# Scores of paged keys run on into the paged-value stage of a hybrid decoder step, with four changes of order

## The chip, the cores and the metric

The kernel runs on one core of one Trainium2 chip. The metric is the device time of one launch in microseconds (us), median of several runs, lower is better. TensorE (PE in the profile) multiplies, VectorE (DVE) and ScalarE (ACT) work element by element, GpSimd (POOL) builds masks, and SyncE (SP) issues nearly all the DMA loads and stores. Each engine works through its own instructions in a fixed order and waits for others by semaphores.

## The reference

One step of one layer. Keys and values of 64 past pages are looked up through a page table; the rest is dense.

```python
def branch_inputs(h, w_in, w_alpha, b_alpha):
    u = h @ w_in                      # 2048 -> q, k, v, gate of 8 heads; q, k, v, gate of 4 GLA heads; rank-16 decay
    log_f = log_sigmoid(ga @ w_alpha + b_alpha) / GLA_TAU

def stick_break_weights(z, mask):
    sp = where(mask, softplus(z), 0.0)
    later = cumsum(sp, reverse=True) - sp
    return where(mask, exp(log_sigmoid(z) - later), 0.0)

def sb_sample(q, k_new, v_new, k_past, v_past, bias):      # 8 requests, 4 new tokens, 1024 past tokens each
    z = concatenate([sb_logits(q, k_past, bias), sb_logits(q, k_new, bias)])
    a = stick_break_weights(z, mask)
    return a[..., :P] @ v_past + a[..., P:] @ v_new

def gla_chunk(S, q, k, v, g):
    ...
def branch_output(o_sb, sg, o_gla, gg, gla_norm_g, w_out):
    mixed = concatenate([o_sb * silu(sg), rms_norm(o_gla) * silu(gg)])
    return mixed @ w_out

# x + rms_norm(branch_output(...)) for 1024 prompt tokens (with 16 learned ones ahead) and for 8 x 4 sample tokens;
# k_past = cache_k[page_table], v_past = cache_v[page_table]: 8 pages of 128 tokens per request, 8 heads of 128
```

## The kernel before, in words

All products are made of three matmuls on values split into a high and a low part. The normalised input, transposed, stays on the chip for the whole run. A projection of 128 output columns (`inproj`) takes eight weight pairs of k-tiles (kk = 0 to 7) by three chunks of tokens. One unit is one chunk of one pair: six matmuls. So a projection has 24 units. Each weight pair is loaded (`wr`), cast to its high part by ScalarE (`wh`) and split into its low part by VectorE (`wl`), each with three buffers: the load of pair i waits for VectorE's split of pair i−3, which waits for TensorE's last matmul of pair i−6.

The stages in order of time: the prologue (to 85 us) loads and transposes the input; eight stick-breaking heads, each with the projections v, k and q and its attention; a low-rank product for the decay; gates 0 to 2; the GLA stage with four heads of k, q and two v projections, then gates 3 and 4 (to some 1503 us); the paged stage, gates 5 to 13 with the products of past values (to some 1750 us); gates 14 and 15; and from some 1800 us the output product, whose 104 weight pieces go through a ring of buffers.

Everything beside a projection is woven between its units by `Weaver` (`W`). A piece of work is a generator; `yield n` puts it aside for n units, `spawn` adds one with a delay. `flush` runs units until no piece is left but those marked lasting, `drain` until none is left at all. The instructions so laid down are then ordered by a scheduler at build time, by priority (weights and evacuations are urgent) and by its own times; what it puts out is the fixed order of each engine. `W.mark` is the last matmul of the latest unit, and a dependency without a semaphore on it (`spread`) keeps an instruction from being ordered ahead of that unit.

`z_feed` makes the scores of the past keys. There are 512 steps, one per head, request and page: a load of 64 KB (`kp`, 128 keys of one head) and four VectorE instructions (`jk`, one for each new token) that multiply with a broadcast query (`qb`) and sum. The number of the page is read from the table on SyncE with a register load ahead of the DMA (`page_dma`). A request's row of eight pages goes out to DRAM (`zd`). In the kernel before one page is taken every 2 units from the heads on, three loads ahead in three buffers, and all are done before the paged stage.

In the paged stage, `chain(b)` reads request b's scores back (`dz`) and makes its stick-breaking weights `dA`; `paged_values` loads its eight pages of values, 512 KB each (`vr`, six buffers, issued four pages ahead), and multiplies them (`dO`). `new_keys` adds the new tokens' own part (`Cs`, `Cn`). A request's products can't start before its scores of all heads are there.

In a head, q is taken out of PSUM by ScalarE (`q`, high part, L620) and, straight from PSUM too, by VectorE (low part, L621); the next projection's first matmuls (`acc_v`, or `acc_ga` after the last head) need the PSUM buffer. In the GLA stage a key tile is transposed by token (`by_token`, tile `tr_k`) and a packed copy of 32 of its columns is transposed too (`packed`, tile `trp_k`, copied out as `pk`), both through one PSUM buffer.

Of the kernel before, what the change touches and what calls it, by code (L numbers as in the profile page):

```python
# [10 lines left out]
F32 = mybir.dt.float32  # L11
F32R = mybir.dt.float32r
# [8 lines left out]
P = 128  # L21
# [29 lines left out]
class Weaver:  # L51
# [3 lines left out]
    def __init__(self):  # L55
        self.now, self.n, self.live, self.heap, self.mark = 0, 0, 0, [], None
# [20 lines left out]
    def drain(self):  # L77
        while self.heap:
            self.beat()
# [3 lines left out]
def hybrid_step(ctx: ExitStack, tc: tile.TileContext, x_prompt, x_sample, cache_k, cache_v, state_gla,  # L83
# [195 lines left out]
    def inproj(c0, evac, lo0, nm, chunks=CHUNKS):  # L279

        acc = [accp.tile([P, 512], F32, tag="acc", name=f"acc_{nm}_{c}") for c in range(3)]
        for kk in range(NK // 2):
            wh, wl = weight_chunk(w_in[0], kk, c0, f"{nm}_{kk}")
            for c, (lo, hi) in enumerate(chunks):
                lo = max(lo, lo0)
                n = hi - lo
                for k2 in range(2):
# [3 lines left out]
                    W.mark = mm(acc[c][:, :n], wl[:, k2, :], hh[k][:, lo:hi], start=False, stop=(k == NK - 1)).ins  # L291
                if kk == NK // 2 - 1:
                    with urgent():
                        evac(c, acc[c][:, :n], lo, hi)
# [32 lines left out]

    dk_cm = tc.tile_pool(name="dk", bufs=2, side="right")
# [17 lines left out]
    heads_ready = []  # L346
    z_done = set()

    def z_feed(rate):
# [8 lines left out]
        def fetch(h, b, i):  # L358
            if i == 0:
                qbs[h, b] = dk.tile([P, NT, P], F32, tag="qb", bufs=2, name=f"qb{b}_{h}")  # L360
                nc.sync.dma_start(qbs[h, b][:], qsd[b * NT:(b + 1) * NT, h * P:(h + 1) * P].partition_broadcast(P))
            kps[h, b, i] = dk.tile([P, P], F32, tag="kp", bufs=3, name=f"kp{b}_{h}_{i}")
# [5 lines left out]
        for n, (h, b, i) in enumerate(pages()):  # L368
            while h not in heads_ready:
                yield 4  # L370
            while fetched < n + 3:
# [7 lines left out]
            if i == 0:  # L379
                zt = dk.tile([P, NT, NPG], F32, tag="zt", name=f"zt{b}_{h}")  # L380
            kp = kps.pop((h, b, i))
            for t in range(NT):
                jk = dk.tile([P, P], F32, tag="jk", bufs=1, name=f"jk{b}_{h}_{i}_{t}")
# [10 lines left out]
    def spread(ins):  # L394

        if W.mark is not None:
            tc.add_manual_dep(ins.ins, W.mark.name, NOSYNC, reason="spread")
# [46 lines left out]
    with tc.tile_pool(name="sp", bufs=1) as sp, tc.tile_pool(name="sps", bufs=1, space=PSUM) as sps:  # L444
# [134 lines left out]
        def head(h):  # L579
# [37 lines left out]
            def ev_q(c, ps, lo, hi):  # L617
                e = min(hi, REAL)
                a, b_, n = lo - META, e - META, e - lo
                act.activation(qt[0][:, a:b_], ps[:, :n], AF.Copy, scale=QSCALE)  # L620
                vec.scalar_tensor_tensor(qt[1][:, a:b_], ps[:, :n], QSCALE, qt[0][:, a:b_].bitcast(F32), ALU.mult, ALU.subtract)  # L621
                if hi > REAL:
                    act.activation(qsm[:], ps[:, n:], AF.Copy, scale=QSCALE)
                    W.spawn(sample_q(h, qsm, ks), 5)
# [4 lines left out]
        W.spawn(z_feed(lambda n: 2), lasting=True)  # L629
# [7 lines left out]
        for g in range(3):  # L637
            gate_group(g)
# [3 lines left out]
    with tc.tile_pool(name="gp", bufs=1) as gp, tc.tile_pool(name="gps", bufs=1, space=PSUM) as gps:  # L642
# [51 lines left out]
        def level_masks():  # L694

            yield 12
            for m in (64, 32, 16, 8, 4, 2, 1):
                nb = P // (2 * m)
                a = stage(f"lv{m}")[:, :P]
# [16 lines left out]
        def decay(g, cb):  # L716

            raw = stage(f"walr{g}")[:96, :P]
            for i in range(6):
# [823 lines left out]
```

## Time and profile before

| | us |
|---|---|
| median of 3 runs | 2154.19 (2152.64 to 2156.18) |
| profiled execution | 2153.79 |
| its span | 2152.1 |
| TensorE busy | 2078.1 (97%) |
| VectorE busy | 1572.5 (73%) |
| ScalarE busy | 993.1 (46%) |
| the 2048 `jk` instructions | 590.5 and 166.1 for reading their sums |
| VectorE busy from 840 to 1500 | 557.25 of 660 |
| VectorE busy from 1540 to 1750 | 86.08 of 210 |

The share of busy time says which engine sets the pace of a stage, and the list of TensorE's waits says what it stood for. The granted clock is given for each stretch of time; at 0.50 TensorE runs at half its speed. A busy row in parentheses has the number of instructions.

### The profile page before, as it was taken

How to read it: one execution, taken by the hardware profiler on the slowest of the kernel's cores; microseconds unless marked ns; L12 is line 12 of the kernel's file. 1: busy time of each engine (PE TensorE's matmuls, PEld its weight loads, DVE VectorE, ACT ScalarE, POOL GpSimd, SP SyncE). 2: the span in 40 equal slices, each digit the busy share in tenths (PEclk: the TensorE clock that was granted, in tenths of full speed). 3: DMA queues.
4: the chain of work that ended last, by engine and by line, in shares of the span. 5: the costliest groups of instructions: out<-in, count | busy, mean ns of one | idle time of the engine just before them, and what ended most of it. 6: DMA issues, size and time to landing. Idle time of an engine off the chain costs nothing.

```text
span 2152.1 us, 43331 instructions
## 1 busy us (share of the span) xinstructions
PE 2078.1 (97%) x12546; PEld 1872.8 (87%) x12546; DVE 1572.5 (73%) x6592; ACT 993.1 (46%) x2536; POOL 83.2 (4%) x298
## 2 busy tenths in 40 slices
PE   5999999999999999999999999999999999999997
PEld 5999999998999979998899898998788887777765
DVE  6368889888898879788788887977544347453575
ACT  7345556564655546432534435343443336332342
POOL 0000010000000010020000000000000000000000
PEclk9999999999999999999999999999999999999999
DMA  6125554554555453442343434335776766452485
GB/s 196 52 70 137 139 158 134 161 146 140 149 152 157 135 142 113 124 100 75 107 106 84 117 80 112 97 83 138 221 228 221 222 200 210 130 158 76 128 277 178
DMA packets 380802, 304.02 MB, mean 141 GB/s; under 512 B 50770, under 2 KB 321042, under 8 KB 380562
## 3 DMA queue, kind: packets, MB, share of 16 engines
q1 hardware_dynamic: 378370, 300.97, 48.0%
q8 instruction: 99, 1.62, 0.3%
q14 instruction: 141, 1.16, 0.2%
q10 hardware_dynamic: 2192, 0.27, 0.1%
HBM read 243.39 MB, written 57.72 MB: 140 GB/s over the span
## 4 chain that ended last, share of the span: by engine, by line
PE 71%; DVE 12%; DMA 10%; ACT 3%; issue 3%; SPq 1%; POOL 0%; DVEq 0%; ACTq 0%; POOLq 0%
DVE jk L384 5%; PE acc_g L289 4%; PE acc_g L291 4%; PE acc_g L290 4%; PE b L1452 4%; PE b L1453 4%; PE b L1454 4%; DMA kp<-in_cache_k_dram 3%; PE acc_k L289 3%; PE acc_k L290 3%; PE acc_k L291 3%; PE acc_gv L289 2%; PE acc_gv L291 2%; PE acc_gv L290 2%; PE acc_q L289 2%
## 5 line engine op out<-in xcount | busy, mean ns | idle before, releaser
L384 DVE SCALAR_TENSOR_TENSOR jk<-kp,qb 128x128 f32<-128x128 f32 x2048 | 590.5, 288 | 90.2 <-DMA kp<-in_cache_k_dram 51.8
L289 PE MATMUL acc_g<-hT,wh_g 128*128 128x304 f32 (+2 forms) x768 | 253.8, 330 | 5.1 <-ACT gx L438 4.7
L291 PE MATMUL acc_g<-hT,wl_g 128*128 128x368 f32 (+2 forms) x768 | 248.0, 323 | 0.0
L290 PE MATMUL acc_g<-hT,wh_g 128*128 128x304 f32 (+2 forms) x768 | 247.9, 323 | 0.0
L289 PEld LDWEIGHTS acc_g<-hT,wh_g 128*128 128x128 f32 x768 | 144.9, 189 | 31.9 <-ACT wh_g L184 12.1
L1452 PE MATMUL b<-ring,f 128*128 128x512 f32 x416 | 165.8, 400 | 3.4 <-ACT b L1351 1.6
L1316 DVE TENSOR_TENSOR ring<-wr,ring 128x512 fp32r<-128x512 f32 x104 | 70.6, 689 | 133.0 <-ACT ring L1315 132.5
L384 DVE DVE_READ_ACCUMULATOR jk<-kp,qb 128x1 f32 x2048 | 166.1, 81 | 0.1
L1453 PE MATMUL b<-ring,f 128*128 128x512 f32 x416 | 162.5, 391 | 0.7 <-DVE ring L1316 0.7
L1454 PE MATMUL b<-ring,f 128*128 128x512 f32 x416 | 162.2, 390 | 0.0
L291 PEld LDWEIGHTS acc_g<-hT,wl_g 128*128 128x128 f32 x768 | 145.0, 189 | 1.6 <-issue 1.6
L290 PEld LDWEIGHTS acc_g<-hT,wh_g 128*128 128x128 f32 x768 | 145.1, 189 | 0.7
L1315 ACT CAST ring<-wr 128x512 fp32r<-128x512 f32 x104 | 64.0, 621 | 162.9 <-DMA wr<-in_w_out_dram 80.9
L512 ACT ACTIVATE X<-X 127x512 f32<-127x512 f32 (+4 forms) x112 | 54.9, 491 | 165.2 <-DVE X L511 165.1
L289 PE MATMUL acc_gv<-hT,wh_gv 128*128 128x384 f32 (+1 forms) x384 | 130.1, 339 | 0.0
L289 PE MATMUL acc_k<-hT,wh_k 128*128 128x378 f32 (+1 forms) x384 | 127.6, 332 | 0.0
L291 PE MATMUL acc_gv<-hT,wl_gv 128*128 128x384 f32 (+1 forms) x384 | 126.0, 328 | 0.0
L289 PE MATMUL acc_q<-hT,wh_q 128*128 128x368 f32 (+2 forms) x384 | 125.4, 326 | 0.0
L290 PE MATMUL acc_k<-hT,wh_k 128*128 128x378 f32 (+1 forms) x384 | 125.4, 326 | 0.0
L291 PE MATMUL acc_k<-hT,wl_k 128*128 128x378 f32 (+1 forms) x384 | 125.2, 326 | 0.0
L290 PE MATMUL acc_gv<-hT,wh_gv 128*128 128x384 f32 (+1 forms) x384 | 125.2, 326 | 0.0
L290 PE MATMUL acc_q<-hT,wh_q 128*128 128x368 f32 (+2 forms) x384 | 123.6, 322 | 0.0
(427 smaller groups left out, 5483.4 us busy)
## 6 DMA issues: line engine op xcount, KB each, us to landing
kp<-in_cache_k_dram SPq DMA_DIRECT2D x512, 64.0 KB
vr<-in_cache_v_dram SPq DMA_DIRECT2D x64, 512.0 KB
qb<-qsd SPq DMA_DIRECT2D x64, 256.0 KB
tf<-in_w_out_dram SPq DMA_DIRECT2D x64, 256.0 KB
td<-tf SPq DMA_DIRECT2D x64, 256.0 KB
wr_g<-in_w_in_dram SPq DMA_DIRECT2D x128, 128.0 KB
wr<-td SPq DMA_DIRECT2D x64, 256.0 KB
wr<-in_w_out_dram SPq DMA_DIRECT2D x48, 256.0 KB
```

Source lines behind the costliest of these rows:

```text
L289: mm(acc[c][:, :n], wh[:, k2, :], hh[k][:, lo:hi], start=(k == 0), stop=False)
L290: mm(acc[c][:, :n], wh[:, k2, :], hl[k][:, lo:hi], start=False, stop=False)
L291: W.mark = mm(acc[c][:, :n], wl[:, k2, :], hh[k][:, lo:hi], start=False, stop=(k == NK - 1)).ins
L384: ins = vec.scalar_tensor_tensor(jk[:], kp[:], 1.0, qbs[h, b][:, t, :], ALU.mult, ALU.mult, accum_out=zt[:, t, NPG - 1 - i:NPG - i])
L512: act.activation(X, X, AF.Exp)
L1315: act.copy(wh, r)
L1316: vec.tensor_tensor(wl, r, wh.bitcast(F32), ALU.subtract)
L1452: mm(bk[:], ah, wh, start=first and k == 0, stop=False, skip_group_check=True)
L1453: mm(bk[:], ah, wl, start=False, stop=False, skip_group_check=True)
L1454: mm(bk[:], al, wh, start=False, stop=last and k == 7, skip_group_check=True)
```

## The change

It has five parts.

1. `z_feed` takes a page at 2, 2, 2, 2, 2, 3 units, 2.17 on average. After the GLA stage only the other pieces are drained (`drain(1)`), and `z_feed` goes on in the paged stage. Its queries, sums and first three page buffers lie in a pool of their own (`zq`); in the paged stage it has eleven page buffers in that stage's pool and loads nine pages ahead. The paged stage ends with `drain`.
2. q leaves PSUM by one ScalarE copy into a staging tile (`qraw`); the split into high and low part is a later piece that reads this tile.
3. `packed` of the keys comes behind `by_token`, with two units between each; `packed` of the values waits two units more. `new_keys` starts at 16 units instead of 10, a chain's product 10 units after its scores instead of 8.
4. A GLA head's decay weights come by one broadcast DMA instead of six, for head 0 already in gate 2. The seven level masks lie in one tile instead of seven staging buffers.
5. The small output loads, and the splits of the first four output weights, are tied to units of the gates beside them.

```diff
     def z_feed(rate):
...
-            kps[h, b, i] = dk.tile([P, P], F32, tag="kp", bufs=3, name=f"kp{b}_{h}_{i}")
+            pl, bufs = pages_in
+            kps[h, b, i] = pl.tile([P, P], F32, tag="kp", bufs=bufs, name=f"kp{b}_{h}_{i}")
...
-            while fetched < n + 3:
+            while fetched < n + (3 if pages_in[0] is zq else 9):
...
+                raw = stage(f"qraw{h}_{c}")
+                act.activation(raw[:, :hi - lo], ps, AF.Copy, scale=QSCALE)
+                W.spawn(split_q(raw, lo - META, e - META, hi - lo))
+
+            def split_q(raw, a, b_, w):
+                n = b_ - a
+                act.copy(qt[0][:, a:b_], raw[:, :n])
+                vec.tensor_tensor(qt[1][:, a:b_], raw[:, :n], qt[0][:, a:b_].bitcast(F32), ALU.subtract)
+                if w > n:
+                    act.copy(qsm[:], raw[:, n:w])
+                    W.spawn(sample_q(h, qsm, ks), 4)
...
-        W.spawn(z_feed(lambda n: 2), lasting=True)
+        W.spawn(z_feed(lambda n: 2 + (n % 6 == 5)), lasting=True)
...
+            if g == 2:
+                W.spawn(first_decay_loads(), 14)
             gate_group(g)
...
-            for i in range(6):
-                nc.sync.dma_start(raw[16 * i:16 * i + 16], w_alpha[0, :, g * P:(g + 1) * P])
+        nc.sync.dma_start(walr[g], bass.AP(tensor=a.tensor, offset=a.offset, ap=[[0, 6]] + [list(d) for d in a.ap]))
...
-            packed(rep_, pk[:], 2, f"k{g}")
             by_token(kt, kd, (0, 4), col, f"k{g}")
-            yield 1
+            yield 2
             by_token(kt, kd, (4, 4), col, f"k{g}")
-            yield 1
+            yield 2
             by_token(kt, kd, (8, 1), col, f"k{g}")
+            yield 2
+            packed(rep_, pk[:], 2, f"k{g}")
...
         for g in range(3, 5):
             gate_group(g)
-        W.drain()
+        W.drain(1)
...
+        pages_in[:] = dp, 11
...
         def new_keys():
-            yield 10
+            yield 16
...
         for g in range(5, 14):
             gate_group(g)
-        W.flush()
+        W.drain()
...
-            nc.sync.dma_start(small[c][:, k, :], md[8 * c + k][:, SEQ:TOUT])
+            spread(nc.sync.dma_start(small[c][:, k, :], md[8 * c + k][:, SEQ:TOUT]))
...
+                if (p, q) == (1, 0) and k < 4:
+                    spread(i, 5 - k)
+                    spread(j, 5 - k)
```

SyncE, before, from the load of gate 6's first weight pair to the first page of values. Names carry gate and pair (`wr_g6_0`), request and page (`vr0_0`), or request, head and page (`kp4_7_1`):

```order
L180 DMA wr_g6_0_27242<-in_w_in_dram 128x2x128
L431 DMA md4_113<-gs4_768_26786 128x304
L389 DMA zd7_92<-zt7_7_26626 128x32
L180 DMA wr_g6_1_27292<-in_w_in_dram 128x2x128
L1206 DMA small0_30181<-md4_113 128x32
L1063 DMA znall_26883<-znd_125 32x256
L1122 DMA dz0_26981<-zd0_85 128x256
L342 ISA
L342 DMA vr0_0_27170<-in_cache_v_dram 128x1024
```

SyncE, changed, the same stretch, cut where pages follow each other in the same form:

```order
L181 DMA wr_g6_0_26831<-in_w_in_dram 128x2x128
L359 TENSOR_LOAD pt_83
L359 ISA x2
L366 ISA
L366 DMA kp4_7_1_26322<-in_cache_k_dram 128x128
...
L366 DMA kp4_7_7_26434<-in_cache_k_dram 128x128
L415 DMA zd3_88<-zt3_7_25997 128x32
L1153 DMA dz0_26472<-zd0_85 128x256
L386 DMA qb5_7_26480<-qsd_84 128x4x128
...
L415 DMA zd4_89<-zt4_7_26493 128x32
L366 DMA vr0_0_26849<-in_cache_v_dram 128x1024
```

In place of six other loads there now stand 16 pages of keys and 11 other loads between the two (gate 6's weight pairs 1 to 5 among them).

SyncE in gate 7, before, between the loads of its weight pairs 5 and 6:

```order
L180 DMA wr_g7_5_27827<-in_w_in_dram 128x2x128
L342 DMA vr1_4_27586<-in_cache_v_dram 128x1024
L421 DMA go6_768_27597<-od6_99 128x272
L342 DMA vr1_5_27644<-in_cache_v_dram 128x1024
L431 DMA md6_115<-gs6_16_27539 128x368
L431 DMA md6_115<-gs6_384_27558 128x384
L180 DMA wr_g7_6_27866<-in_w_in_dram 128x2x128
```

In the changed kernel 13 pages (8 of keys, 5 of values), a query load and five others stand there, and vr1_4 comes later.

TensorE, changed, gate 7 (`acc_g7_0` and `acc_g7_1` are its first two chunks, `hT5` the sixth k-tile, so pair 2):

```order
L1123 MATMUL dO0_26893<-vr0_6_27045,dA0_26724 32x512 x2
L290 MATMUL acc_g7_0_27449<-hT5_152,wh_g7_2_27616 128x368
L291 MATMUL acc_g7_0_27449<-hT5_152,wh_g7_2_27616 128x368
L292 MATMUL acc_g7_0_27449<-hT5_152,wl_g7_2_27617 128x368
L1123 MATMUL dO0_26893<-vr0_7_27099,dA0_26724 32x512 x2
L1207 MATMUL dO0_26893<-vn_26272,an_26271 32x256 x4
L1217 MATMUL oT0_27531<-ident_73,osb0_27478 128x128 x4
L1123 MATMUL dO1_27480<-vr1_0_27176,dA1_27200 32x512 x2
L1123 MATMUL dO1_27480<-vr1_1_27239,dA1_27200 32x512 x2
L290 MATMUL acc_g7_1_27450<-hT0_147,wh_g7_0_27454 128x384
```

Before, request 0 ends ahead of gate 7's first matmul, and dO1's first pages stand behind pair 1 of all chunks; now both stand behind pair 2 of the first chunk and ahead of pair 0 of the second.

More of the change, by code (lines that the diff above doesn't have):

```diff
@@ L75, in flush, with drain @@
             self.beat()
-    def drain(self):
-        while self.heap:
+    def drain(self, keep=0):
+        while len(self.heap) > keep:
             self.beat()
@@ L716, in decay @@
         def decay(g, cb):
[L718 to L728 removed]
+            if g:
+                decay_loads(g)
+            raw = walr.pop(g)
             yield 6
```

64 lines of the change are left out of this document (37 added, 27 removed).

## The prediction

> **What bounds the kernel now.** I read the page's busy shares first, then the busy time stage by stage, then what TensorE waited for, then single clock windows, and at the end the DMA queue that SyncE issues.
>
> ```profile
> PE 2078.1 (97%) x12546; PEld 1872.8 (87%) x12546; DVE 1572.5 (73%) x6592; ACT 993.1 (46%) x2536; POOL 83.2 (4%) x298
> 85.00:840.00 755.00, 742.54 (x4460) 700.82 (x4459) 627.94 (x2888) 411.61 (x1050) 58.75 (x202) 0.99 0.49 136
> 840.00:1500.00 660.00, 643.62 (x4219) 604.46 (x4219) 557.25 (x2882) 282.48 (x804) 19.13 (x68) 0.99 0.39 103
> 1500.00:1540.00 40.00, 36.79 (x208) 32.25 (x208) 22.03 (x66) 15.21 (x36) 2.45 (x11) 0.91 0.67 204
> 1540.00:1750.00 210.00, 210.00 (x1390) 179.12 (x1389) 86.08 (x205) 78.41 (x181) 0.00 (x0) 1.00 0.67 213
> ```
>
> The columns of the last four rows are the stretch, its length, then the busy time of TensorE, its weight loads, VectorE, ScalarE and GpSimd, the granted clock, the DMA share and GB/s. TensorE bounds every stage. In the heads (85 to 840) it is idle 12.5 us, in the GLA stage (840 to 1500) 16.4 us, at the entry to the paged stage 3.2 us, and in the paged stage itself not at all: 210.0 of 210.0. VectorE is 84% busy in the GLA stage and 41% in the paged stage. So the change takes VectorE work out of stages where TensorE waits 2% of the time and puts it where TensorE has no slack; both ends have to be priced.
>
> ```profile
> PE acc_g L289 <- ACT gx L438: 4.7, 2, 2.4
> PE z L526 <- ACT hi_s L490: 3.9, 6, 1.9
> PE acc_ga L315 <- DVE q L621: 3.5, 1, 3.5
> PE trp_v L857 <- ACT gv L873: 3.1, 1, 3.1
> PE tr_k L868 <- DVE pk L860: 3.0, 4, 0.7
> PE z L527 <- DVE lo_s L491: 2.9, 8, 1.4
> PE al L740 <- DMA kp<-in_cache_k_dram: 2.7, 1, 2.7
> PE acc_v L289 <- DVE q L621: 2.7, 3, 1.5
> PE acc_gk L289 <- ACT gx L438: 2.4, 1, 2.4
> PE Cs L1105 <- issue: 1.6, 1, 1.6
> ...
> PE C L1135 <- ACT dc_h L1054: 1.0, 1, 1.0
> PE b L1452 <- ACT ring L1315: 0.8, 2, 0.5
> PE b L1453 <- DVE ring L1316: 0.7, 3, 0.2
> ```
>
> These are TensorE's waits after 85 us: total, times, longest. Each is small, but an idle stretch has an after-effect:
>
> ```profile
> 787.80:791.23 3.43, 1.26 (x9) 1.02 (x7) 1.15 (x7) 0.48 (x2) 0.00 (x0) 1.00 0.83 267
> 791.24:798.06 6.82, 5.49 (x21) 3.07 (x22) 6.12 (x32) 2.75 (x11) 0.21 (x1) 0.50 0.54 160
> 525.00:528.40 3.40, 1.48 (x8) 0.96 (x6) 3.06 (x11) 2.91 (x7) 0.65 (x2) 1.00 0.51 159
> 528.41:531.82 3.41, 3.20 (x11) 2.84 (x11) 3.27 (x16) 1.84 (x4) 0.83 (x1) 0.50 0.23 63
> 907.29:910.70 3.41, 3.41 (x14) 3.41 (x13) 2.10 (x13) 0.59 (x2) 0.00 (x0) 0.50 0.80 249
> 920.95:924.35 3.40, 2.95 (x9) 2.98 (x10) 2.15 (x14) 1.63 (x3) 3.21 (x15) 0.50 0.49 132
> 996.04:999.44 3.40, 3.40 (x14) 3.40 (x13) 2.46 (x9) 0.30 (x2) 0.00 (x0) 0.50 0.28 75
> 1511.45:1514.86 3.41, 3.41 (x13) 3.04 (x13) 2.53 (x7) 1.57 (x4) 0.00 (x0) 0.50 0.63 237
> 1531.93:1535.34 3.41, 3.41 (x15) 1.48 (x14) 0.84 (x2) 1.08 (x2) 0.00 (x0) 0.50 0.31 112
> 405.55:408.95 3.40, 1.89 (x13) 1.65 (x12) 3.40 (x13) 1.12 (x3) 0.00 (x0) 1.00 0.77 229
> ```
>
> About 2 us of idle inside one 3.41-us stretch (525.0: 1.48 busy of 3.40) brings a clock of 0.50 in the next; 1.5 us of idle (405.55) did not. A stretch at 0.50 loses half of itself, 1.7 us. So a wait of over about 1.7 us costs nearly double.
>
> The Trainium skill, "TensorE: Matmul & The Clock Gate", section "What's actually happening", has the same free-running window of 3413 ns, but says that the clock drops after at least one idle window. By that rule waits of 2 us would cost no clock, and the clock terms below would all be nothing, gains and losses alike. The rows at 525.0 and 528.41 disagree with it, and I go by the rows.
>
> **The paged keys.** A page of scores is one load on SyncE and four pairs on VectorE. The rows are from the page's costliest groups, SyncE's and ScalarE's timeline, and the chain of waits:
>
> ```profile
> L384 DVE SCALAR_TENSOR_TENSOR jk<-kp,qb 128x128 f32<-128x128 f32 x2048 | 590.5, 288 | 90.2 <-DMA kp<-in_cache_k_dram 51.8
> L384 DVE DVE_READ_ACCUMULATOR jk<-kp,qb 128x1 f32 x2048 | 166.1, 81 | 0.1
> 1488.40 1.50 SPq L342 DMA_DIRECT2D kp<-in_cache_k_dram  x2
> 1495.74 0.40 SPq L180 DMA_DIRECT2D wr_g<-in_w_in_dram  x1
> 1496.23 0.42 SPq L911 DMA_DIRECT2D od<-gst_s  x1
> 1767.12 0.41 ACT L184 CAST wh_g<-wr_g 128x256 fp32r<-128x256 f32 x1 [2.45 <-PE acc_g L290]
> 1769.98 0.41 ACT L184 CAST wh_g<-wr_g 128x256 fp32r<-128x256 f32 x1 [2.45 <-PE acc_g L290]
> 1563.46 0.99 PE dO L1092 x8
> ...
> 1592.46 0.99 PE dO L1092 x8
> ```
>
> A pair is 288 + 81 = 369 ns, a page 1.48 us of VectorE. On SyncE two page loads in a row take 1.50 us and one issue of them 0.34, so a page steps by 1.16 us (number load, register work, issue); a plain load steps by 0.48 (1495.74 to 1496.23). A pair of k-tiles of a gate takes TensorE 2.86 us (1767.12 to 1769.98). In the paged stage a gate with its values takes 29.0 us (1563.46 to 1592.46).
>
> **Gains, term by term.**
>
> 1. The evacuation of q. ScalarE copies the three chunks out of PSUM and the split comes later, so the next user of the accumulator no longer waits for VectorE: acc_ga 3.5 + acc_v 2.7 = 6.2. The double stretch at 791.24 goes with the first, half of 6.82 = 3.4. Against it stands one cast more before z can start; bounds are 0 (hidden) and 8 heads by the 0.4 to 0.5 us of one such operation, 3 to 4; I take 3, since z already waits behind its neighbours. Together −6.6.
> 2. trp_k moved behind the by-token transposes: tr_k's wait of 3.0 goes, since the transposes no longer stand behind the copy of trp_k. −3.0.
> 3. Late pages. The waits of al (2.7), acc_gk (2.4) and trp_v (3.1) come from VectorE standing on a page that SyncE issued late, with ScalarE's in-order work behind it: 8.2, and three halved stretches (907, 921, 996) 5.1, together 13.3. A page each 2.17 units instead of 2 lightens both queues by 8%, and five 16-row decay loads less per head of GLA save 5 × 0.48 = 2.4 us of SyncE each. Bounds: nothing (three buffers there remain) and 13.3. I take 0.6 of it: −8.0.
> 4. acc_g behind gx, 4.7 in two places. One follows the crowded end of the GLA stage, the other a wait for an output tile that the change leaves: half, −2.4.
> 5. z behind hi_s and lo_s: 6.8 and the stretch at 528 1.7; these gain only by the lighter VectorE: a third, −2.8.
> 6. Entry to the paged stage: Cs 1.6, C 1.0, two halved stretches 3.4, in all 6.0. The chains start 2 to 6 units later, so their inputs are there. I keep 1 back: −5.0.
> 7. Start of the output product: b behind ring 1.5; the casts are now spread over the last gate's units. −1.2.
>
> Sum −29.0. The single mask tile and the spread small loads have no row to act on at TensorE: 0.
>
> **Losses in the paged stage.** 153 of the 2048 pairs, 38 pages, come to lie there: 153 × 0.369 = 56.5 us of VectorE in about 3.5 gates. At 44 pairs a gate that is 16.2 us on top of the 41% of 29.0 = 11.9: 28.1 of 29.0. VectorE is as good as full for some 100 us, and all of its work is in order, the splits of the gates' weights included. SyncE's queue:
>
> - Between the loads of gate 6's first weight and vr0_0, the first page of values, stand 16 pages and 11 other loads where there were none and six: 16 × 1.16 + 11 × 0.48 = 23.9 us. That weight's buffer comes free five k-pairs before gate 6 starts, so its load issues at −5 × 2.86 + 1.2 = −13.1 at the earliest, and vr0_0 at +10.8. In the chain of waits a page of values takes 3.7 us to land:
>
> ```profile
> 1509.56 3.74 DMA vr<-in_cache_v_dram
> ```
>
>  so it is there at +14.5. TensorE reaches its dO after three k-pairs and a first part, +9.6. Stall 4.9. With it goes everything behind dO on TensorE: it is in order, so gate 6 itself stands.
> - Gates 6 and 7 give SyncE 17 pages and 17 others, then 22 pages and 18 others: 27.9 + 34.2 = 62.1 us against 2 × 29.0 = 58.0 on TensorE. The backlog of 4.1 shows at the last pages of request 0 and the first of request 1 (vr0_7, vr1_0, vr1_1), which are now ahead of two thirds of gate 7's first units. 4.1.
> - Two of these stalls are long enough for a halved stretch: 3.4.
> - VectorE at 97%: the nearest row is the GLA stage at 84%, with 16.4 of 660 us of TensorE idle, 2.5%. Of 115 us that is 2.9, and one halved stretch 1.7: 4.6.
>
> Sum +17.0. Bounds: 6, if the eleven buffers let SyncE run ahead during gate 5 so that only vr0_0 is late; 35, if TensorE waits for late weights in each k-pair, since a late page then stops VectorE, its split, the weight buffer and so the next weight's load on SyncE.
>
> The Trainium skill, "DMA: Bandwidth & Descriptors", section "Latency and other measured facts", puts a floor of about 600 ns on a number load (`tensor_load`). This speaks against the change: with 0.6 for the 0.27 seen here a page would be 1.5 us, and gate 7's 22 pages would need 7 us more. The row decides for the smaller:
>
> ```profile
> L335 SPq TENSOR_LOAD <-pt x576: 261/269/799, 42.4 to 1722.1; - x192
> ```
>
> **Sum.** −29.0 + 17.0 = −12.0. The profiled execution took 2153.79 us (span 2152.1 and 1.7 around it), and the median of the runs is 2154.19, so the two are one: 2153.8 − 12.0 = 2141.8, forecast 2142.
>
> **Rivals.**
>
> - SyncE and VectorE become the bound of the paged stage (slower). Place: from gate 6's first weight to gate 8's. Price: the bound of 35 above, while the late-page term (8.0) and item 6 (5.0) come back too because they belong to the same queues: −16 + 35 = +19, about 2173; it decides from a loss of 29 on, where the gains are used up. For it: 28.1 of 29.0 and 62.1 against 58.0. Against it: nine pages of prefetch, and the excess lasts two gates only. Chance 0.21.
> - SyncE keeps ahead. Then the paged stage costs the low bound and all late-page waits go: −29.0 − 5.3 + 6 = −28, about 2126. For it: gate 5 asks SyncE for 10 pages and 26 others, 24.1 us of 29.0, so it could run 4.9 ahead. Against it: a load waits for its buffer, and the weights' three buffers hold those behind them in SyncE's order. Chance 0.18.
> - The change doesn't do what it says: the waits in the heads and the GLA stage move to other pages, as three buffers stay there and VectorE is still near 80%. Then items 3, 4 and 5 (13.2) are gone, and 2154 to 2156 comes out. Chance 0.17.
>
> **How the numbers follow.** The forecast has what is left, 0.44, with its own range of 2133 to 2150 (the half ways to the bounds of items 3 and 5 and of the loss). The range over all cases is 2124 to 2160: it leaves out the far part of the slower rival, and a little below. A measurement here can tell 0.2%, 4.3 us. Faster by more: all of the forecast but its upper end (0.40), the second rival (0.18), a little of the third (0.03): 0.61. Within: most of the third (0.12), the upper end of the forecast (0.04), the lower of the first (0.01): 0.17. Slower: the rest of the first (0.20) and of the third (0.02): 0.22.
>
> **What would show it.** Right: no wait of acc_ga or acc_v for q; no tr_k for pk; TensorE full at 790 to 800; in the paged stage TensorE waits of 2 to 5 us at dO for vr, once in gate 6 and in gate 7, with a halved stretch behind each, and VectorE over 85% busy there. Wrong: no TensorE idle between 1540 and 1750 (second rival), waits of acc_g for wl_g or wr_g in each k-pair there (first), or al, acc_gk and trp_v waits of the same sum at other places (third). The forecast falls if the paged stage's loss lies outside 6 to 29 us.

## The result, and the profile after

The changed kernel takes 2202.53 us (median of 5 runs, 2201.14 to 2205.15) where the kernel before takes 2153.47 beside it: a ratio of 1.0233, interval 1.0219 to 1.0247. It is 49 us slower; 2142 was forecast, and the range ended at 2160.

The page and TensorE's waits after 85 us (total, times, longest) of the changed kernel:

```profile
PE 2099.0 (95%) x12546; PEld 1882.4 (85%) x12546; DVE 1573.2 (71%) x6592; ACT 1005.9 (46%) x2560; POOL 82.7 (4%) x298
PE C L1164 <- ACT ds_h L1085: 7.9, 3, 4.3
PE z L553 <- DVE lo_s L517: 6.4, 12, 1.6
PE acc_g L292 <- DVE wl_g L186: 5.9, 3, 4.5
...
PE dO L1123 <- DMA vr<-in_cache_v_dram: 5.4, 5, 2.2
```

Several waits that the change was to take are gone (acc_ga and acc_v behind q, al behind a late page); acc_gk behind gx is not, it has grown from 2.4 to 5.1 us. C behind ds_h, acc_g behind wl_g, dO behind vr and z behind q (3.3) weren't there before, and z behind lo_s has doubled. TensorE is busy 21 us longer for the same 12,546 matmuls. Up to half of that is the clock: after 85 us, the very end of the run left out, twelve stretches stand at 0.50, two of them double, where before it was seven, one double. By half of 3.41 each, an estimate from above, that is 24 us lost instead of 14.

Where the time went is read from the first and last start of groups that both kernels have. Of the kernel before:

```profile
L315 PE MATMUL acc_ga<-hT,wa x48: 297/333/528, 792.6 to 813.9; 128*32 128x384 f32 x32, 128*32 128x304 f32 x16
L289 PE MATMUL acc_gk<-hT,wh_gk x192: 297/336/522, 902.6 to 1327.7; 128*128 128x384 f32 x128, 128*128 128x304 f32 x64
L1092 PE MATMUL dO<-vr,dA x256: 592/617/1063, 1523.1 to 1751.2; 128*32 128x512 f32 x128
L1452 PE MATMUL b<-ring,f x416: 387/389/503, 1801.6 to 2115.5; 128*128 128x512 f32 x139
```

And of the changed one:

```profile
L317 PE MATMUL acc_ga<-hT,wa x48: 297/333/365, 796.6 to 816.5; 128*32 128x384 f32 x32, 128*32 128x304 f32 x16
L290 PE MATMUL acc_gk<-hT,wh_gk x192: 296/336/619, 914.6 to 1340.3; 128*128 128x384 f32 x128, 128*128 128x304 f32 x64
L1123 PE MATMUL dO<-vr,dA x256: 592/617/1057, 1546.3 to 1796.8; 128*32 128x512 f32 x128
L1487 PE MATMUL b<-ring,f x416: 387/389/505, 1849.9 to 2165.3; 128*128 128x512 f32 x139
```

| point of the program | later by, us |
|---|---|
| low-rank product, first and last matmul | 4.0 and 2.6 |
| GLA stage, first matmul of gk | 12.0 |
| its last gk projection | 12.6 |
| first product of values | 23.2 |
| last product of values | 45.6 |
| output product, first and last | 48.3 and 49.8 |

So there are two jumps: some 9 us between 816 and 915 us, and 33 us between 1340 and 1797; another 4 come behind. In the heads 7.7 us are lost up to the last matmul of q (796.2 against 788.5), and 3.7 come back with the wait of acc_ga that is gone; the GLA stage takes as long as before up to its last gk projection. In both a gain was forecast.

**The jump in the paged stage.** TensorE and SyncE of the changed kernel in gates 6 and 7, by their timelines (start, duration, engine, then idle time and releaser in brackets):

```profile
1534.03 0.58 PE L1164 MATMUL C<-ds_h,ntri 128*128 128x256 f32 x1 [4.32 <-ACT ds_h L1085]
1546.29 1.05 PE L1123 MATMUL dO<-vr,dA 128*32 128x512 f32 x4
...
1574.65 0.33 PE L292 MATMUL acc_g<-hT,wl_g 128*128 128x368 f32 x1
1576.15 0.62 PE L1123 MATMUL dO<-vr,dA 128*32 128x512 f32 x2 [1.17 <-DMA vr<-in_cache_v_dram]
...
1579.69 1.05 PE L1123 MATMUL dO<-vr,dA 128*32 128x512 f32 x4 [0.71 <-DMA vr<-in_cache_v_dram]
1582.92 1.63 PE L1123 MATMUL dO<-vr,dA 128*32 128x512 f32 x4 [2.18 <-DMA vr<-in_cache_v_dram]
1584.49 0.69 PE L290 MATMUL acc_g<-hT,wh_g 128*128 128x384 f32 x1
1528.94 0.43 SPq L1153 DMA_DIRECT2D dz<-zd  x1
...
1572.81 0.33 SPq L366 DMA_DIRECT2D vr<-in_cache_v_dram  x1
...
1576.21 0.33 SPq L366 DMA_DIRECT2D vr<-in_cache_v_dram  x1
1577.31 0.33 SPq L366 DMA_DIRECT2D kp<-in_cache_k_dram  x1
1578.48 0.33 SPq L366 DMA_DIRECT2D vr<-in_cache_v_dram  x1
```

In these rows of gate 7 SyncE issues a page each 1.1 to 1.2 us; one or two pages of keys stand between two of values, so a page of values comes after 3.4 (1572.81 to 1576.21) and 2.3 us. TensorE goes from the last matmul of a chunk at 1574.65 to the first of the next at 1584.49 through the end of request 0 and the first pages of request 1, and waits for vr0_7, vr1_0 and vr1_1: 1.17 + 0.71 + 2.18 = 4.1 us. This is a place of the prediction, with its mechanism and its size. The other place isn't there: the first dO starts at 1546.29 without a wait. TensorE had stood 4.32 us before, at request 0's C, which waits for the chain whose load dz was issued at 1528.94, behind pages in the same queue.

The waits for vr, 5.4 us in all, are the smaller part of the 33. From the last gk projection to the last dO TensorE is idle 22.9 us instead of 6.8, and 6.6 of these 16 more are waits for C. Its matmuls take 17 us longer. About 7 of that is in acc_g; four more stretches at half speed would make as much. Another 9 are in dO. There are 256 records for 64 pages, so four a page. In the kernel before, the two pages of a pair follow each other, eight records in a row:

```profile
1563.39 1.06 PE L1092 MATMUL dO<-vr,dA 128*32 128x512 f32 x8
```

In the changed kernel, as its TensorE order shows, a pair is torn apart where its loads stand apart in SyncE's order, and the four records of one page take as long (1.05 us at 1546.29). All dO<-vr together are busy 35.0 us before and 43.0 in the changed kernel.

**The jump before the GLA stage.** VectorE's waits between 880 and 925 us of the changed kernel, and TensorE's from 885:

```profile
DVE lvl L744 <- POOL lv L741: 7.7, 6, 2.7
PE acc_g L292 <- DVE wl_g L186: 5.4, 2, 4.5
```

In the kernel before, VectorE casts the seven level masks at 923.6 to 933.2, as GpSimd makes them, with 1.3 us of wait. With one tile instead of seven staging buffers the casts come at 897.1 to 905.9 in VectorE's order, while GpSimd is still at them; they wait 7.7 us, and the low part of gate 2's last weights stands behind (wl_g at 899.6 and 907.2). The prediction had this part at nothing.

### The profile page after: what moved, and what is told of

It is laid out like the page before. It is cut to its first block, busy times and chain, and to the rows that moved or that the text cites. A ratio compares the mean times of both kernels' runs of the same rounds, so it can differ in the third digit from the quotient of the medians.

```text
span 2202.4 us, 43303 instructions
## 1 busy us (share of the span) xinstructions
PE 2099.0 (95%) x12546; PEld 1882.4 (85%) x12546; DVE 1573.2 (71%) x6592; ACT 1005.9 (46%) x2560; POOL 82.7 (4%) x298
## 3 DMA queue, kind: packets, MB, share of 16 engines
q14 instruction: 141, 1.16, 0.2%
## 4 chain that ended last, share of the span: by engine, by line
PE 66%; DVE 12%; DMA 12%; ACT 4%; issue 3%; SPq 2%; POOL 1%; DVEq 0%; ACTq 0%; POOLq 0%
DVE jk L410 5%; PE b L1487 4%; PE acc_g L290 4%; PE b L1488 4%; PE b L1489 4%; DMA kp<-in_cache_k_dram 3%; PE acc_g L291 3%; PE acc_g L292 3%; PE acc_k L290 3%; PE acc_k L291 3%; PE acc_k L292 3%; PE acc_gv L290 2%; PE acc_q L290 2%; PE acc_gv L291 2%; PE acc_gv L292 2%
## 5 line engine op out<-in xcount | busy, mean ns | idle before, releaser
L290 PE MATMUL acc_g<-hT,wh_g 128*128 128x384 f32 (+2 forms) x768 | 258.2, 336 | 6.7 <-ACT gx L464 5.6
L292 PE MATMUL acc_g<-hT,wl_g 128*128 128x384 f32 (+2 forms) x768 | 251.6, 328 | 5.9 <-DVE wl_g L186 5.9
L291 PE MATMUL acc_g<-hT,wh_g 128*128 128x384 f32 (+2 forms) x768 | 250.9, 327 | 0.0
L290 PEld LDWEIGHTS acc_g<-hT,wh_g 128*128 128x128 f32 x768 | 147.8, 192 | 37.0 <-issue 23.1
L291 PEld LDWEIGHTS acc_g<-hT,wh_g 128*128 128x128 f32 x768 | 147.8, 192 | 1.1 <-issue 0.4
L292 PE MATMUL acc_q<-hT,wl_q 128*128 128x368 f32 (+2 forms) x384 | 123.5, 322 | 0.0
```

Source lines behind the costliest of these rows:

```text
L290: mm(acc[c][:, :n], wh[:, k2, :], hh[k][:, lo:hi], start=(k == 0), stop=False)
L291: mm(acc[c][:, :n], wh[:, k2, :], hl[k][:, lo:hi], start=False, stop=False)
```

## The experiments

All were timed beside the kernel before on the same chip; its median there was 2145.8 to 2149.2 us, so ratios and differences to it are compared, not times.

**Undoing the overrun, and the overrun alone.**

```diff
-        W.spawn(z_feed(lambda n: 2 + (n % 6 == 5)), lasting=True)
+        W.spawn(z_feed(lambda n: 2), lasting=True)
...
-        W.drain(1)
+        W.drain()
```

> The changed kernel with part 1 undone: a page every 2 units again, all pages done before the paged stage; parts 2 to 5 stay. Theory A (the overrun fills SyncE's queue in the paged stage and costs about 27 us there, 1515 to 1650 us): about 2173 us, and no TensorE wait at dO for vr after 1500. Theory B (the loss lies in the changes of order, whatever the pages do): 2195 us or more. Under both the VectorE wait for the masks near 900 us stays.

2178.21 us, 1.0143 (1.0124 to 1.0161): 32 slower than before. No wait for vr is left, and from the last gk projection (1347.4) to the last dO (1772.5) the kernel takes 425.1 us, where the changed one takes 456.5 and the kernel before 423.5. So in the paged stage the overrun costs 31 us; ahead of it it gains, and over the whole kernel it costs about 0.9% (19 us). 32 us of loss have nothing to do with it. Neither theory alone holds.

> The kernel before with part 1 alone: a page each 2.17 units, running on into the paged stage with eleven buffers and nine loads ahead. Theory A: 2175 to 2185 us, with TensorE waits at dO for vr one page step (2.3 us) apart near 1575 us. Theory B: within 5 us of 2154.

(The edit is part 1 of the change on the kernel before.) 2170.45 us, 1.0105 (1.0088 to 1.0123): 25 us slower. Its profile has the waits for vr at dO:

```profile
PE dO L1099 <- DMA vr<-in_cache_v_dram: 8.4, 6, 2.5
PE C L1140 <- ACT ds_h L1061: 8.2, 3, 5.9
L290 PE MATMUL acc_gk<-hT,wh_gk x192: 297/336/445, 895.1 to 1313.0; 128*128 128x384 f32 x128, 128*128 128x304 f32 x64
L1099 PE MATMUL dO<-vr,dA x256: 592/617/1059, 1514.9 to 1767.4; 128*32 128x512 f32 x128
1540.00:1640.00 100.00, 87.96 (x510) 66.86 (x510) 58.07 (x261) 32.80 (x74) 0.00 (x0) 0.97 0.69 215
```

The kernel before, profiled beside the later experiments:

> The kernel before, profiled on the same chip as the three that follow, since chips differ by some microseconds. It should show no TensorE wait between 1540 and 1750 us.

```profile
L289 PE MATMUL acc_gk<-hT,wh_gk x192: 297/336/522, 898.8 to 1324.4; 128*128 128x384 f32 x128, 128*128 128x304 f32 x64
L1092 PE MATMUL dO<-vr,dA x256: 592/617/1062, 1518.8 to 1746.8; 128*32 128x512 f32 x128
1540.00:1640.00 100.00, 100.00 (x668) 84.96 (x667) 47.72 (x113) 43.23 (x99) 0.00 (x0) 1.00 0.71 229
```

It took 2151.68 us, and TensorE waits for nothing from 1540 to 1640. Against it the overrun gains 11.4 us up to the last gk projection (1324.4 to 1313.0), is still 3.9 ahead at the first dO and 20.6 behind at the last. The lighter pace does pay ahead of the paged stage, as items 3 and 5 had it (10.8). From there to the last dO it loses 11.4 + 20.6 = 32 us; TensorE does 510 matmuls in 100 us where it did 668, and its dO are busy 44.3 us instead of 35.0.

**Which of VectorE and SyncE.** Leaving out three of four VectorE pairs of each late page:

```diff
+                if h == HEADS - 1:
+                    pool.memset(zt[:], 0.0)
...
-            for t in range(NT):
+            for t in range(NT if pages_in[0] is zq else 1):
```

> The overrun alone, leaving out three of the four VectorE pairs of each page scored in the paged stage (those scores stay zero); the page loads on SyncE are all there. Theory A: still 15 to 25 us slower than the kernel before, with the same waits at dO for vr. Theory E: not more than 5 us slower, and no such waits.

2170.46 us, 1.0115 (1.0091 to 1.0138): the same as with all pairs, though VectorE now has less to do than in the kernel before:

```profile
1540.00:1640.00 100.00, 90.11 (x512) 67.45 (x512) 40.50 (x129) 32.43 (x73) 0.25 (x2) 0.95 0.70 216
```

512 matmuls with VectorE busy 40.5 us, 510 with 58.1, and TensorE still waits 5.8 us for vr at dO. VectorE is not the bound.

Moving the late pages to GpSimd's queue:

```diff
-    def page_dma(dst, cache, b, i, hs):
+    def page_dma(dst, cache, b, i, hs, eng=None):
...
-            page_dma(kps[h, b, i][:], cache_k, b, i, slice(h, h + 1))
+            page_dma(kps[h, b, i][:], cache_k, b, i, slice(h, h + 1), nc.sync if pages_in[0] is zq else nc.gpsimd)
```

> The overrun alone, with the page loads that fall into the paged stage (number load and DMA) issued by GpSimd, which is idle there, instead of SyncE; nothing is left out, VectorE's work is the same. Theory A (SyncE is the bound there): the 38 us lost between 1515 and 1620 us fall to 10 or less, and with the 14 us gained before it the kernel comes out 0 to 12 us faster than the one before. Theory E (VectorE, with its 150 more pairs, is the bound): 20 us or more slower, as with the overrun alone.

2172.08 us, 1.0126 (1.0094 to 1.0157): no better, and against the expectation of theory A. Its profile says why. All waits for vr and for the chains' C are gone, but GpSimd needs 2.44 us a page (1492.24 to 1494.68), and the masks that new_keys waits for (made at 1502.6 to 1503.2) stand behind pages in its queue:

```profile
PE Cs L1113 <- issue: 18.7, 1, 18.7
1492.24 0.54 POOL L347 DMA_DIRECT2D kp<-in_cache_k_dram  x1 [2.01 <-issue]
1494.68 0.54 POOL L347 DMA_DIRECT2D kp<-in_cache_k_dram  x1 [1.90 <-issue]
```

One bound was replaced by a slower one, so this run alone settles nothing. Two other runs settle it: they leave VectorE's work and the pages' bytes as they are and change only what SyncE has to do for them. In the first the page number is taken as fixed:

```diff
+            if pages_in[0] is zq:
+                page_dma(kps[h, b, i][:], cache_k, b, i, slice(h, h + 1))
+            else:
+                nc.sync.dma_start(kps[h, b, i][:], cache_k[0, b * NPG + i:b * NPG + i + 1, :, h:h + 1, :].rearrange("o p h d -> p (o h d)"))
```

> The overrun alone, with the page loads of keys in the paged stage taken from a fixed page each instead of the page table's (so these scores come from other pages): the number load and register work of some 35 pages are left out, the DMAs, their bytes and VectorE's work stay. Theory A (SyncE's step of 1.16 us a page is what the paged stage waits for): a late page then steps by about 0.5 us, some 20 us less of SyncE in gates 5 to 8, and the 35 to 38 us lost there fall below 18: at most 5 us slower than the kernel before. Theory F (the place of request 0's chain and of the first values behind the page loads costs it, whatever a load takes): 15 us or more slower.

2152.84 us, 1.0019 (1.0007 to 1.0031): 4 us slower instead of 25. The same bytes, the same DMAs, the same VectorE work; only number loads and their register work are gone, so the traffic itself isn't what costs. The second is the same move to ScalarE's queue, with nothing left out:

> The overrun alone, with the number loads and DMAs of the pages loaded in the paged stage issued by ScalarE (40% busy there) instead of SyncE; nothing is left out. Theory A (SyncE's full queue is the cause): no TensorE wait for a page of values, and 0 to 10 us slower than the kernel before, as with fixed pages (4 us), where the overrun alone is 25 slower. Rival H (ScalarE's evacuations and casts stand behind the page loads, as VectorE stood behind GpSimd's): 15 us or more slower, with waits for gx or wh.

2145.30 us against 2148.18, 0.9991 (0.9979 to 1.0003). The 25 us are gone:

```profile
L347 ACTq DMA_DIRECT2D kp<-in_cache_k_dram x41: 339/348/402, 1469.1 to 1566.8; - x41
1547.96 1.68 ACTq L347 DMA_DIRECT2D kp<-in_cache_k_dram  x2
PE acc_g L290 <- ACT gx L445: 1.8, 2, 1.5
PE oT L1194 <- ACT osb L1187: 1.4, 1, 1.4
1540.00:1640.00 100.00, 96.84 (x636) 82.38 (x636) 62.23 (x263) 36.80 (x84) 0.00 (x0) 1.00 0.74 234
```

The two PE rows are all of TensorE's waits from 1540 to 1640, and it does 636 matmuls there, with VectorE busier (62.2 us) than with the overrun on SyncE. Two pages in a row step by 1.68 − 0.35 = 1.33 us on ScalarE, slower than on SyncE, but beside the pages of values, not between them. The dO are busy 34.1 us again, so the pairs are whole. From the last gk projection (1314.4) to the last dO (1742.4) 428.0 us pass, against 454.4 with the pages on SyncE and 422.4 in the kernel before: 26 of the 32 us are gone, and of the other 6 a wait of 3.4 at Cs is the largest part. That is theory A shown: what the overrun cost was, for the most part, its page loads in SyncE's queue. The queue isn't full in the sense that SyncE never stands: with the overrun alone it waits 27 of the 100 us from 1540 to 1640, 21 of them for VectorE with a load of weights at its head. What costs is the place and the length of the page loads in a fixed order.

**Less overrun.** One extra unit in 12 pages, and in 24:

> The overrun alone at a page each 2.08 units (one extra unit in 12 pages, not in 6), so that 108 pairs (27 pages) and not 184 follow the first of the paged stage in VectorE's order. By SyncE's counts gates 6 and 7 then need 33 pages x 1.16 + 36 others x 0.48 = 55.6 us against 58. Theory A: the queue just fits, the loss there falls to 10 or so, and with half the gain ahead of it the kernel lies within 5 us of the one before. Theory F: the loss falls only in part, 10 to 18 us slower.

> As the one before with one extra unit in 24 pages (71 pairs late; gates 6 and 7 need 25 pages x 1.16 + 34 x 0.48 = 45 us of SyncE). Theory A: no TensorE wait for a page of values; 0 to 6 us faster than the kernel before. Theory F: 5 to 12 us slower, from request 0's chain at the entry.

2169.81 us, 1.0098 (1.0081 to 1.0114), and 2162.78, 1.0069 (1.0048 to 1.0089). In the paged stage itself TensorE loses far less, as theory A has it, though not as little as its counts said: from the last gk projection to the last dO 16 and 8 us more than without an overrun (to 1764.4 and 1757.0), where some 10 and no wait were expected. At 2.04 no wait for a page of values is left.

```profile
1540.00:1640.00 100.00, 96.12 (x600) 78.28 (x599) 48.61 (x149) 39.10 (x89) 0.00 (x0) 1.00 0.73 227
1540.00:1640.00 100.00, 97.93 (x625) 81.23 (x625) 44.17 (x105) 38.88 (x88) 0.00 (x0) 1.00 0.71 226
L290 PE MATMUL acc_gk<-hT,wh_gk x192: 297/336/522, 902.8 to 1325.8; 128*128 128x384 f32 x128, 128*128 128x304 f32 x64
L290 PE MATMUL acc_gk<-hT,wh_gk x192: 297/336/522, 904.6 to 1327.0; 128*128 128x384 f32 x128, 128*128 128x304 f32 x64
```

(The rate of 2.08 first in each pair, then 2.04.) 600 and 625 matmuls against 510. But the gain ahead of it is gone altogether: the last gk projection starts at 1325.8 and 1327.0, later than without an overrun (1324.4), not 11 earlier. Both expected times were missed for that. The gain doesn't grow with the pace; why 2.17 has it and 2.08 not stays open. It also shows how far such an edit reaches: the whole order is laid down anew at each build, and a pace between two others moved this point by some 12 us. Costs of 7 to 10 us of single parts, below, are of that size, and where no wait carries them the order alone may.

**The masks.**

```diff
-            lv = xtile("lv")
-            for i, m in enumerate((64, 32, 16, 8, 4, 2, 1)):
+            for m in (64, 32, 16, 8, 4, 2, 1):
...
-                a = lv[:, i * P:(i + 1) * P]
+                a = stage(f"lv{m}")[:, :P]
```

> The changed kernel with the seven level masks back in seven staging buffers; nothing else differs. Theory C (VectorE's casts of the masks, put early by the one tile, wait 7.7 us for GpSimd near 900 us, and the gate's weight split stands behind them: 5.5 us of TensorE, 3 us at the next stage's start and two halved stretches of clock): 2190 to 2195 us. Rival: VectorE only waits for late pages there instead, and it stays within 4 us of 2202.

1.0202 (1.0178 to 1.0226) in place of 1.0233: 7 us less, with intervals that touch. Its time of 2188.3 lies below what was expected because that chip was quicker (the kernel before took 2145.8); in proportion it is some 2196, a little less gain than expected. The profile is plainer: from 885 to 925 us acc_g's wait for wl_g (5.4) is gone, and VectorE waits for no mask there. From the last matmul of the low-rank product to the first of gk it takes 90.4 us (810.4 to 900.8), the changed kernel 98.1 and the kernel before 88.7, so nearly the whole first jump goes with the masks.

**The split of q.** Part 2 alone on the kernel before:

> The kernel before with part 2 alone: q leaves PSUM by one ScalarE copy and is split later. As predicted (6.2 us of waits and 3.4 of clock gone, 3 of new z waits): 2147 us. Theory D (z's first matmuls wait for the split that now comes later, 1 to 2 us in a head, some with a halved stretch, as in the changed kernel's heads, which lost 8 us by 790 us): 2153 to 2160 us, with z waits of 8 us or more in the heads.

2162.02 us, 1.0073 (1.0049 to 1.0097): 16 us slower (10 to 21 by the interval), more than theory D had, where a gain of 6.6 was predicted. TensorE's waits in its heads:

```profile
PE z L526 <- ACT hi_s L490: 8.5, 8, 2.9
PE z L506 <- DVE q L626: 7.4, 5, 2.6
```

The waits of acc_v and acc_ga for q are gone, as forecast. In their place z waits 7.4 for the low part of q, and twice as long for hi_s; with 3.1 for lo_s z waits 19.0 us in the heads, against 5.6 in the kernel before profiled on that chip. The profiled executions are 7.9 us apart, and the low-rank product starts 7.4 later (797.2 against 789.8), so the loss arises in the heads. Two more runs asked what of this is the cost. The split made urgent:

```diff
-                act.copy(qt[0][:, a:b_], raw[:, :n])
...
+                with urgent():
+                    act.copy(qt[0][:, a:b_], raw[:, :n])
+                    vec.tensor_tensor(qt[1][:, a:b_], raw[:, :n], qt[0][:, a:b_].bitcast(F32), ALU.subtract)
```

> Part 2 alone, with the split of q at the same urgent priority as the copy out of PSUM. Theory D (the split of q, put behind other work of ScalarE and VectorE, is what z waits for): the z waits for q fall from 7.4 us to under 3, and the kernel lies within 5 us of the one before instead of 16 above. Rival (the third copy through ScalarE itself costs it): 10 us or more above, as with part 2 alone.

2163.97 us, 1.0081 (1.0056 to 1.0105): no change; z still waits 6.7 for q. A higher priority doesn't bring the split earlier. And the attention started four units later:

```diff
-            W.spawn(attend(h, qt, kt, V), 2)
+            W.spawn(attend(h, qt, kt, V), 6)
```

> Part 2 alone with a head's attention started 6 units after its q projection, not 2. Theory D (z's first matmuls only meet a split that is 1 to 3 us late): the z waits for q fall under 1.5 us, and of the 16 us at least 8 go. If it stays at 12 us or more above the kernel before, the cost of part 2 isn't in that wait, but in what the split pushes back on ScalarE and VectorE (hi_s, lo_s).

2169.33 us, 1.0099 (1.0078 to 1.0120): slower still. The wait for q is gone from its list, but:

```profile
PE z L526 <- ACT hi_s L490: 15.0, 12, 1.7
PE z L527 <- DVE lo_s L491: 6.8, 15, 0.9
```

So the wait for the split alone isn't the 16 us; with it out of the way more is waited for inside the attention. That part 2 costs, and that the z waits carry it, is shown; whether through the third pass of ScalarE or through the order it brings is not.

**The moves of packed.** On the kernel before:

```diff
-            packed(rep_, pk[:], 2, f"k{g}")
             by_token(kt, kd, (0, 4), col, f"k{g}")
...
+            packed(rep_, pk[:], 2, f"k{g}")
...
             if c == 2:
+                yield 2
                 packed(rep, pv[:, f * P:(f + 1) * P], 1, f"v{g}_{f}")
```

> The kernel before with the moves of packed alone (behind the by-token transposes for the keys, two units later for the values). As predicted: the tr_k waits of 3.0 us go, 2 to 4 us faster. Rival G (the wait only moves: trp_k then stands behind the copies of the next transposes, and trp_v's wait grows, 7.1 and 6.8 us in the changed kernel without the overrun): 3 to 10 us slower.

2155.20 us, 1.0031 (1.0021 to 1.0041): 7 us slower.

```profile
PE trp_k L858 <- DVE pv L861: 6.9, 4, 3.2
PE trp_v L858 <- ACT gv L874: 6.6, 4, 3.2
```

The tr_k waits of 3.0 are gone. Four waits of trp_k and three more of trp_v stand there, 13.5 us where the kernel before had 6.1. The 7.4 us more are about the loss. Rival G holds: one PSUM buffer serves them all, and whichever comes second waits.

**What is left of the change.**

> The changed kernel without the overrun, q, masks and packed: what is left are the decay loads, the later new_keys and chains, and the spread loads and splits at the end. If the parts add up (32 without the overrun, less 16 for q, 7.5 for the masks, 6.6 for packed): +2 us, from 4 faster to 5 slower. The predicted gain of entry and output start (6 us) would show as 5 faster or more.

(The changed kernel with parts 1 and 2, the masks and packed undone.) 2159.49 us, 1.0047 (1.0031 to 1.0063): 10 us slower (7 to 14 by the interval), more than expected. Its waits:

```profile
PE trp_v L877 <- ACT gv L893: 9.1, 4, 3.1
L290 PE MATMUL acc_gk<-hT,wh_gk x192: 297/336/620, 895.5 to 1328.1; 128*128 128x384 f32 x128, 128*128 128x304 f32 x64
```

trp_v now waits four times and not once (3.6 us in the kernel before on the other chip), and the last gk projection starts 3.7 us late (1328.1 against 1324.4). Of what is left of the change only the decay loads and the pool `zq` touch that stage. From 1500 to 1545 us there is no TensorE wait at all, where the kernel before has 3.4: the later new_keys and chains do what item 6 said. Behind that the kernel falls back again; the waits of acc_g for gx are 8.7 us in seven places (3.6 in two in that profile of the kernel before). Which of the remaining parts does that wasn't tried.

> The changed kernel without the late split of q, without the one mask tile and without the moves of packed, and with the late pages' loads issued by ScalarE. If the four causes found (the late pages on SyncE, q, masks, packed) are all of the 49 us, nothing slows it and the gain ahead of the paged stage is left: 5 us faster to 4 slower than the kernel before. If another part costs, or ScalarE's queue does: 8 us or more slower.

(The same with the overrun, its pages on ScalarE's queue.) 2163.33 us, 1.0060 (1.0040 to 1.0081): 15 us slower. The four causes found were not all; the rest costs about what it cost without the overrun (10). The five single costs, 1.05, 0.73, 0.31, 0.31 and 0.47%, add up to 2.87%, the change to 2.33. Each is known to some 0.1 to 0.3%, so it can't be told whether they overlap.

**A version from it.** The overrun with its pages on ScalarE's queue, and the one line of part 3 that item 6 rests on:

> The overrun with its late pages on ScalarE's queue, and new_keys at 16 units instead of 10 (one line of part 3). With the pages on ScalarE TensorE still stands 3.4 us at Cs near 1486 us, and a doubled halved stretch follows (another 3.4). If Cs then finds its inputs ready: 3 to 8 us faster than the kernel before. If the wait only moves to Cn or a chain's C: within 3 us of it.

2147.10 us against 2149.20, 0.9991 (0.9982 to 1.0000). The wait at Cs is gone, but a chain's C now waits 7.0 us for the copy of Cs, on ScalarE. It moved. Both versions are about 2 us faster than the kernel before by their medians, which can't be told from no change (both intervals reach 1), and some 50 faster than the changed one.

## Why the prediction was wrong

Between 2142 and the 2202.5 measured lie 61 us. Some 16 of them are in the paged stage, where 17 were forecast and 33 came; the other 45 are in the items that were counted as gains of 29 and cost 16.

- **Paged stage, +17.0.** SyncE's 1.16 us a page was right, and so was the backlog of 62.1 − 58.0 = 4.1 us: vr0_7, vr1_0 and vr1_1 are waited for 4.1 us in gate 7. The step that failed is to price the loss by waits for vr at dO alone. Those were 9.0 in the sum and 5.4 in the run; the stall of 4.9 at vr0_0 isn't there. Left out were the chain of request 0, whose load dz stands in the same queue (C waits 7.9 us for ds_h, 4.3 of it here, with a double stretch at half speed behind it), and the pairs of pages that the new order tears apart (dO busy 43.0 us instead of 35.0). The trace also has 15 pages between gate 6's first weight and vr0_0, not 16, which takes 1.2 us off the count. The upper bound of 35 was near the loss, but "late weights in each k-pair" was the wrong reason for it: in that stage acc_g waits once for wl_g, 0.5 us.
- **VectorE at 97%, +4.6.** Fell. With a quarter of the late pairs nothing changes. Read the busy row, not the sum: with the overrun alone VectorE was 58% busy there (58.07 of 100 us). It waited little for pages (0.6 us); it stood most for ScalarE's cast of weights (12.6), for oT (8.4) and for a load of go (8.4).
- **Item 1, −6.6.** The waits went, as said. The step that failed is the term of 3 for z, bounded by 4: with part 2 alone z waits 13.4 us more in the heads (19.0 against 5.6), and the kernel is 16 us slower. The bound "8 heads by one operation" counted the extra cast alone; z waits up to 2.6 us at a time for the low part of q and 2.9 for hi_s, which is more than one operation. What puts these late stays open.
- **Item 2, −3.0.** tr_k's wait went and two others came: +7 us. The step took a wait off one user of a shared buffer and didn't ask who has it next.
- **Items 3 and 5, −10.8.** With the overrun alone 11.4 us are gained by the last gk projection. That the size agrees is partly luck: al's wait for a page went (4.6) and trp_v's fell from 3.6 to 0.5, but acc_gk's stayed (1.9 and 2.4), 6.0 of the 11.4 come in the heads (783.8 against 789.8 at the low-rank product), where item 5 had 2.8, and at 2.08 units there is no gain.
- **The masks, 0.** They cost about 7 us by two intervals that touch, and 7.7 by the stretch in the two profiles. "No row to act on" was wrong: in the kernel before, and with the staging buffers back, the casts come late enough for GpSimd.
- **Item 6, −5.0.** Shown without the overrun (no wait left from 1500 to 1545). In the changed kernel the wait is at C instead.
- **Item 7, −1.2, and the decay loads (in item 3).** Item 7 isn't seen: b waits 1.1 + 0.7 for ring, as against 0.8 + 0.7. The decay loads, with the rest of parts 3 to 5, cost 10 us instead of gaining; which of them does is open.
- **The rivals.** The first, at a chance of 0.21 and a price of 2173, came true in place, in SyncE and in the size of the paged stage's loss, not in VectorE nor in its sign. It is 30 us short, because it kept 16 us of the other items' gains. The third, waits that move to other places, holds for items 1 and 2, but was priced at no more than the gains lost.
- **The clock.** By the Trainium skill ("TensorE: Matmul & The Clock Gate", section "What's actually happening") a wait of 2 us would cost no clock. The trace disagrees, as in the kernel before: in the changed kernel the stretch from 1583.32 on is at half speed behind the wait of 2.2 at 1582.92, less than a whole window. By the estimate above the clock took up to 10 of the 49 us.

```profile
1579.90:1583.30 3.40, 1.22 (x6) 0.14 (x4) 1.56 (x5) 2.15 (x6) 0.00 (x0) 0.99 0.67 200
1583.32:1586.70 3.38, 3.38 (x11) 2.22 (x8) 0.00 (x0) 0.41 (x1) 0.00 (x0) 0.50 0.54 118
```

## What to carry to other kernels

Work that is moved to a stage brings its DMA issues with it: count the queue's steps per unit of the stage it goes to, number loads and register work included, and ask what else stands in the same queue, and what order of the other engines follows from it; an engine that looks full by a sum may be only waiting. A wait behind a shared buffer, or a cast behind another engine, is kept off by the order around it; when that order changes, each such pair has to be read again. Changes of order should be tried one at a time: here each of the five pieces, timed singly, came out slower, the masks at the edge of what can be told.

## What the runs showed of the hardware

The step of a page load depends on the engine that issues it: 1.1 to 1.2 us on SyncE, 1.33 on ScalarE, 2.44 on GpSimd, for the same number load, register work and DMA. Of SyncE's step the number load is 0.27 and the DMA issue 0.34; a load without a number steps by 0.48. The eight dO records of two pages take 1.06 us when they follow each other (kernel before, 1563.39), the four of one page alone 1.05 (changed kernel, 1546.29).
